# Probabilities transposed by 32x32 blocks on VectorE and by DMAs, with the attention stage in an order written out by hand

## The chip, the cores and the metric

The kernel runs on one NeuronCore of a Trainium2 chip, as one program. The metric is the device time of one execution in microseconds (us), shown as the median of several runs. Weights and activations come from the chip's main memory in 32-bit floats. The core's engines are PE (TensorE, matmuls and transposes), DVE (VectorE), ACT (ScalarE), POOL (GpSimd) and SP (SyncE, which here only issues DMAs). Each runs its own instruction list in order, and they wait for one another by semaphores.

## What is computed

Two encoder layers on `x` of shape (512, 1024). Three token mixers run side by side on one input projection, are scaled by gates and summed; an output projection, LayerNorm, a squared-ReLU MLP and a second LayerNorm follow.

```python
for layer in range(2):
    qa, ka, va, qb, kb, vb, qc, kc, vc, gate_logits = split(x @ w_in[layer])
    oa = dilated_attention(partial_rotary(qa) * scale, partial_rotary(ka), va)      # A: 4 heads of 64
    ob = axial_gqa(axial_rotary(rms_norm(qb)) * scale, axial_rotary(rms_norm(kb)), vb)   # B: 8 query heads, 2 k/v heads
    oc = neighbourhood_attention(qc * scale, kc, vc, rpb_c[layer])                  # C: 4 heads, 8 x 64 grid
    g = sigmoid(gate_logits + b_gate[layer])                                        # three gates of 1024
    mix = (g0 * (oa @ w_branch_a) + g1 * (ob @ w_branch_b) + g2 * (oc @ w_branch_c)) @ w_out
    x = layer_norm(ALPHA * x + mix)
    x = layer_norm(ALPHA * x + square(relu(x @ w_up)) @ w_down)
```

## The kernel before

**Matmuls.** Every operand is kept as a rounded part `hi` and a rest `lo` of 32-bit type fp32r, and `mm3` (lines 153 to 155) makes a product of three passes, hi*hi, hi*lo and lo*hi. Weights arrive in tiles of 128x1024 (`raw`, line 194). `Stream.split` makes `whi` on ACT (line 182) and `wlo = raw - whi` on DVE (line 183). Two `raw` tiles and up to five (in later stages eight) split tiles exist at a time, and `take` hands out the next one and advances the stream.

**The attention stage.** `attention` projects the queries and keys of mixer A, and then opens the stage that this case is about. Its outer loop runs over 64 *slots* a layer: 16 heads (four of A, four of C, eight of B) times four blocks `qb` of 128 queries. A slot has one block of scores, softmax, the transposition of its probabilities, and once a head the product with the values. Into each slot `work.pump(rate)` puts a share of matmuls that don't hang on it, twice: the projections of B and C, all gates of A and C, and the branch projections of A and C. So PE always has filler work. `rate` (2.1 for A, 2.85 for C, 1.6 for B) is the number of `mm3` of 512 columns that one call puts in. `chores` are pieces of head preparation (`prepare`, `norm_rotate`), of which `chores.pump` emits one or two at a time. Instructions of this stage are ordered by the framework's scheduler, from the order of the code.

**One slot.** `scores` (lines 513 and 514) multiplies q by the two parts of k into a bank `pss`. For A and C line 523 adds mask or bias and takes the maximum on DVE; for B line 519 does so by a reduction. Line 524 negates the maximum, line 525 is the exponential on ACT, line 528 the reciprocal of the sum on DVE, and line 529 scales the probabilities `p` by it, on POOL for A and B and on DVE for C. `turn` (line 544) transposes `p` in up to four 128x128 blocks on PE, by a product with `ident`, into a bank `psp`. `split_psum` (lines 228 and 229) writes `pth` on ACT and `ptl = psp - pth` on DVE. When the head's four slots are through, `values` (lines 558 and 559) multiplies the values by both parts. C's blocks see 256 or 384 keys, the others 512.

**Heads.** The matmul of the scores wants q split over both halves of the partitions (its `hi` in one, its `lo` in the other), and k whole in both halves. `head_k` (lines 446 and 447) writes both halves of `kh` on ACT and of `kl` on DVE, from the bank in which PE has transposed k.

**After the slots**, `tail` runs the gates and the projection of branch B, with the last head's `values` inside the first gate. Then come the output projection and the MLP, whose code the change leaves as it is but for the pool in which each weight tile is put.

PSUM has eight banks, dealt round by the pool: whatever bank is next is waited for, by `return psum.tile([P, 512], F32, tag="ps", name=name)`.

## Time and profile before

| | |
|---|---|
| median of 3 runs | 1547.56 us (1546.23 to 1547.92) |
| the profiled execution: its own time | 1549.4 us |
| its span, first to last instruction | 1547.6 us |
| busy: PE / DVE / ACT / POOL | 99% / 56% / 41% / 12% of the span |
| instructions | 19148 |
| DMA traffic | 150.61 MB, 97 GB/s over the span |

The span is what the rows below divide; 1.8 us of the execution lie outside it. An engine's idle time matters only where PE comes to wait for it. Matmuls overlap: one of 512 columns is shown with some 0.39 us, but the next starts 0.23 us later. The chain of waits counts each by what it adds.

### The profile page before, as it was taken

How to read it: one execution, taken by the hardware profiler on the slowest of the kernel's cores; microseconds unless marked ns; L12 is line 12 of the kernel's file. 1: busy time of each engine (PE TensorE's matmuls, PEld its weight loads, DVE VectorE, ACT ScalarE, POOL GpSimd, SP SyncE). 2: the span in 40 equal slices, each digit the busy share in tenths (PEclk: the TensorE clock that was granted, in tenths of full speed). 3: DMA queues.
4: the chain of work that ended last, by engine and by line, in shares of the span. 5: the costliest groups of instructions: out<-in, count | busy, mean ns of one | idle time of the engine just before them, and what ended most of it. 6: DMA issues, size and time to landing. Idle time of an engine off the chain costs nothing.

```text
span 1547.6 us, 19148 instructions
## 1 busy us (share of the span) xinstructions
PE 1527.6 (99%) x7400; PEld 1279.8 (83%) x7400; DVE 866.0 (56%) x1498; ACT 632.5 (41%) x1036; POOL 182.0 (12%) x190
## 2 busy tenths in 40 slices
PE   8999999999999999999999999999999999999997
PEld 6888888888898888888888888888888888888886
DVE  4678877644664314441566787776448542244315
ACT  4665666533144212431136556665332431134310
POOL 0113213211100000000102141233111000000001
PEclk9999999999999999999999999999999999999999
DMA  6222311153153323332331323112432432233311
GB/s 218 83 85 75 111 55 58 52 177 123 55 177 96 96 82 96 110 96 83 106 128 56 98 82 103 55 59 95 146 123 83 136 99 92 82 123 95 96 55 55
DMA packets 43434, 150.61 MB, mean 97 GB/s; under 512 B 5072, under 2 KB 5712, under 8 KB 43344
## 3 DMA queue, kind: packets, MB, share of 16 engines
q1 hardware_dynamic: 43344, 149.40, 30.5%
q8 instruction: 58, 0.95, 0.2%
q14 instruction: 32, 0.26, 0.1%
HBM read 145.19 MB, written 4.19 MB: 97 GB/s over the span
## 4 chain that ended last, share of the span: by engine, by line
PE 95%; DVE 2%; ACT 1%; DMA 1%; issue 0%; POOL 0%; SPq 0%; POOLq 0%; DVEq 0%; ACTq 0%
PE psd L155 9%; PE psd L154 9%; PE psd L153 9%; PE psu L154 8%; PE psu L155 8%; PE psu L153 8%; PE psg L155 6%; PE psg L154 6%; PE psg L153 6%; PE psp L544 3%; PE psq L155 2%; PE psq L153 2%; PE psq L154 2%; PE psb L155 2%; PE psb L153 2%; PE psb L154 2%
## 5 line engine op out<-in xcount | busy, mean ns | idle before, releaser
L183 DVE TENSOR_TENSOR wlo<-raw,whi 128x1024 fp32r<-128x1024 f32 (+1 forms) x246 | 306.9, 1248 | 421.5 <-ACT whi L182 420.5
L182 ACT ACTIVATE whi<-raw 128x1024 fp32r<-128x1024 f32 (+1 forms) x246 | 258.4, 1053 | 462.8 <-PE psd L155 143.1
L153 PE MATMUL psu<-xTh,whi 128*128 128x512 f32 (+1 forms) x576 | 210.8, 366 | 0.0
L154 PE MATMUL psu<-xTl,whi 128*128 128x512 f32 (+1 forms) x576 | 210.7, 366 | 0.0
L155 PE MATMUL psu<-xTh,wlo 128*128 128x512 f32 (+1 forms) x576 | 210.5, 365 | 0.0
L153 PE MATMUL psd<-whi,hh 128*128 128x512 f32 x512 | 199.3, 389 | 0.0
L155 PE MATMUL psd<-whi,hl 128*128 128x512 f32 x512 | 199.2, 389 | 0.0
L154 PE MATMUL psd<-wlo,hh 128*128 128x512 f32 x512 | 199.2, 389 | 0.0
L153 PE MATMUL psg<-xTh,whi 128*128 128x512 f32 x384 | 156.8, 408 | 0.0
L154 PE MATMUL psg<-xTl,whi 128*128 128x512 f32 x384 | 151.6, 395 | 0.0
L155 PE MATMUL psg<-xTh,wlo 128*128 128x512 f32 x384 | 151.6, 395 | 0.0
L154 PEld LDWEIGHTS psu<-xTl,whi 128*128 128x128 f32 x576 | 108.6, 189 | 17.7
L153 PEld LDWEIGHTS psu<-xTh,whi 128*128 128x128 f32 x576 | 108.6, 189 | 17.4
L155 PEld LDWEIGHTS psu<-xTh,wlo 128*128 128x128 f32 x576 | 108.6, 189 | 17.4
L266 POOL TENSOR_TENSOR ve<-ve,nhalf 128x1 f32<-128x1 f32 x16 | 24.2, 1513 | 775.0 <-DVE ve L265 775.0
L529 POOL TENSOR_SCALAR p<-p,stat 128x512 f32<-128x512 f32 x96 | 70.7, 737 | 360.2 <-DVE stat L528 242.9
L154 PEld LDWEIGHTS psd<-wlo,hh 128*128 128x128 f32 x512 | 96.1, 188 | 20.0
L153 PEld LDWEIGHTS psd<-whi,hh 128*128 128x128 f32 x512 | 96.1, 188 | 19.9
L155 PEld LDWEIGHTS psd<-whi,hl 128*128 128x128 f32 x512 | 96.1, 188 | 19.8
L153 PE MATMUL psq<-whi,xTh 128*128 128x512 f32 (+1 forms) x256 | 90.0, 351 | 7.2 <-ACT whi L182 6.7
L229 DVE TENSOR_TENSOR ptl<-psp,pth 128x512 fp32r<-128x512 f32 (+2 forms) x128 | 81.6, 637 | 21.2 <-ACT pth L228 19.8
L155 PE MATMUL psq<-whi,xTl 128*128 128x512 f32 (+1 forms) x256 | 87.9, 343 | 0.0
(116 smaller groups left out, 2572.7 us busy)
## 6 DMA issues: line engine op xcount, KB each, us to landing
raw<-in_w_up SPq DMA_DIRECT2D x64, 512.0 KB, 3.6
raw<-in_w_down SPq DMA_DIRECT2D x64, 512.0 KB, 3.5
raw<-in_w_gate SPq DMA_DIRECT2D x48, 512.0 KB, 3.5
raw<-in_w_qkv SPq DMA_DIRECT2D x22, 512.0 KB, 3.6
raw<-in_w_out SPq DMA_DIRECT2D x16, 512.0 KB, 3.6
raw<-in_w_c SPq DMA_DIRECT2D x12, 512.0 KB, 3.5
bias<-in_rpb SPq DMA_DIRECT2D x8, 640.0 KB, 3.9
raw<-in_w_bb SPq DMA_DIRECT2D x8, 512.0 KB, 3.6
```

The costliest lines, as they stand in the source:

```text
L153: nc.tensor.matmul(ps, lhs.hi, rhs.hi, start=start, stop=False)
L154: nc.tensor.matmul(ps, lhs.hi, rhs.lo, start=False, stop=False)
L155: nc.tensor.matmul(ps, lhs.lo, rhs.hi, start=False, stop=stop)
L182: nc.scalar.activation(hi[:, s], raw[:, s], AF.Copy)
L183: nc.vector.tensor_tensor(lo[:, s], raw[:, s], f32(hi[:, s]), op=ALU.subtract)
L229: nc.vector.tensor_tensor(dst.lo, ps, f32(dst.hi), op=ALU.subtract)
L266: nc.gpsimd.tensor_tensor(ve[:, 1:], ve[:, :1], nhalf[:, :1], op=ALU.pow)
L529: (nc.vector if name == "c" else nc.gpsimd).tensor_scalar(p, p, st[:, 3:4], 1.0, op0=ALU.mult, op1=ALU.mult)
L544: nc.tensor.transpose(ps[:, j * P:(j + 1) * P], p[:, j * P:(j + 1) * P], ident)
```

## The change

Probabilities are no longer transposed on PE. `turn` has DVE transpose each 32x32 block of `p` where it stands (one instruction a slot, into a tile `tx`), and `gather` moves the blocks to their partitions by 16 DMAs a head, each of 32 rows of 2 KB. The order of the 512 queries inside the result becomes (i, q, b), so `chosen`, `values` and `evict` use strided views. The tile that lands is the exact transposed matrix, so `settle` makes `hi` from it on ACT, in SBUF, and subtracts it in place on POOL (in the last head of a layer by turns on DVE). A head is settled two heads after it was scored, and its values are multiplied at the end of that time.

`head_k` writes one half only, and two DMAs copy it to the other. q and k are prepared head by head. The softmax takes the maximum negated, so line 524 goes; C's probabilities are scaled on POOL as the others. PSUM banks are dealt in groups by name: two for scores, three for `psk` and `psc`, three for the rest. The attention stage and the tail are emitted under `manual_schedule`, in the order of the code: `later`, `chain` and `catch_up` put PSUM evictions and the stream's splits at places in each slot. The rates become 2.2, 2.5 and 1.75. Split weight tiles are four (`AHEAD`) in each of two pools; the second pool is used in the first projection and by turns from the output projection on, so that the attention stage has four tiles instead of five. Of the plan of weights, the first tiles of C come ahead of B's k and v. The core of the diff:

```diff
-    psum = ctx.enter_context(tc.tile_pool(name="psum", bufs=8, space=bass.MemoryType.PSUM))
+    GROUPS = {"pss": (0, 2), "psk": (2, 5), "psc": (2, 5), None: (5, 8)}
...
+    def catch_up():
+        todo = soon[:]
+        soon.clear()
+        for f in todo:
+            f()
+        for c in chain[:]:
+            if next(c, None) is None:
+                chain.remove(c)
+        stream.advance()
...
-            for i in (h, 1 - h):
-                to = slice(i * HD, (i + 1) * HD)
-                nc.scalar.activation(dst(k.hi[to]), src(ps[own]), AF.Copy)
-                nc.vector.tensor_tensor(dst(k.lo[to]), src(ps[own]), dst(f32(k.hi[own])), op=ALU.subtract)
+            nc.scalar.activation(dst(k.hi[own]), src(ps[own]), AF.Copy)
+            yield 1
+            nc.vector.tensor_tensor(dst(k.lo[own]), src(ps[own]), dst(f32(k.hi[own])), op=ALU.subtract)
+            yield 1
+            for t in (k.hi, k.lo):
+                nc.sync.dma_start(f32(t)[other], f32(t)[own])
...
-            ps = bank("psp")[:, :n * P]
-            for j in range(n):
-                nc.tensor.transpose(ps[:, j * P:(j + 1) * P], p[:, j * P:(j + 1) * P], ident)
-            split_psum(pt[:, k0:k1, qb * P:(qb + 1) * P], ps.rearrange("p (k q) -> p k q", q=P))
+            nc.vector.transpose(squares[name, h][1][:, :, k0:k1, qb].rearrange("p j k b -> p k j b"),
+                                p.rearrange("p (k j a) -> p k j a", j=4, a=SQ))
+
+        def gather(name, h, ms, queues=(nc.sync,)):
...
+            for m in ms:
+                i, j = m % 4, m // 4
+                queues[m % len(queues)].dma_start(f32(lo)[j * SQ:(j + 1) * SQ, i],
+                                                  sq[i * SQ:(i + 1) * SQ, j].rearrange("a k q b -> a k (q b)"))
...
+        def settle(name, h, kbs, engines=(nc.gpsimd, nc.gpsimd)):
...
+            for kb in kbs:
+                q = keys_of(name, kb)
+                hi, lo = chosen(pt.hi[:, :, kb], *q), chosen(pt.lo[:, :, kb], *q)
+                nc.scalar.activation(hi, f32(lo), AF.Copy)
+                engines[kb % 2].tensor_tensor(lo, f32(lo), f32(hi), op=ALU.subtract)
...
-        rate = {"a": 2.1, "c": 2.85, "b": 1.6}
+        rate = {"a": 2.2, "c": 2.5, "b": 1.75}
...
+        with tc.manual_schedule():
...
+            for i, (name, h, qb) in enumerate(slots):
+                if i + 1 < len(slots):
+                    todo[i + 1].normalize()
+                score(i + 2)
+                turn(name, h, qb, todo[i].p)
+                if i >= 2 * TB and qb < 3:
+                    settle(*head_of(i - 2 * TB), ((0, 1), (2,), (3,))[qb])
+                catch_up()
+                soften(i + 2)
+                chores.pump()
+                work.pump(rate[name])
+                catch_up()
+                if i >= 2 * TB and qb == 3:
+                    values(*head_of(i - 2 * TB))
...
+                if i >= TB - 1:
+                    at = (i + 1) % TB
+                    gather(*head_of(i - at), range(4 * at, 4 * at + 4))
...
+            gather(*head_of(-1), range(4, 16), (nc.sync, nc.scalar))
+            settle(*head_of(-1 - TB), range(TB))
```

Over the two layers the program loses 464 transposes on PE, 128 subtractions `ptl`, 128 negations and 32 scalings of C on DVE, and 20 half copies of k each on ACT and DVE. It gains 128 block transposes on DVE, 124 subtractions, 32 scalings of C and 32 small fills of `tx` on POOL, 500 gathers and 40 copies of k among SP's DMAs, 12 gathers issued by ACT, and eight more evictions of C's outputs each on ACT and DVE.

How rows move, at three places of the B heads in the first layer. First PE, before, in one slot; `psb` is a branch projection, `psp` the transposition:

```order
L153 MATMUL psb_2665<-oh_1639,whi_2238 128x512 [waits PE_49]
L154 MATMUL psb_2665<-ol_1640,whi_2238 128x512
L155 MATMUL psb_2665<-oh_1639,wlo_2239 128x512
L544 MATMUL psp_2671<-ident_73,p_2587 128x128 [waits Pool_49]
L544 MATMUL psp_2671<-ident_73,p_2587 128x128 x3
L153 MATMUL psb_2665<-oh_2023,whi_2238 128x512
L154 MATMUL psb_2665<-ol_2024,whi_2238 128x512
L155 MATMUL psb_2665<-oh_2023,wlo_2239 128x512
```

And PE now, at the end of a head's last slot, `psg` being a gate's projection and `pso` the values of the head before the last:

```order
L184 MATMUL psg_2453<-xTh_80,whi_2268 128x512
L185 MATMUL psg_2453<-xTl_81,whi_2268 128x512
L186 MATMUL psg_2453<-xTh_80,wlo_2269 128x512
L646 MATMUL pso_2512<-pth_2402,v_808 128x512 [waits DVE_49,PE_49]
L646 MATMUL pso_2512<-ptl_2231,v_808 128x512 [waits DMAHW4_49,DMAHW3_49,DMAHW5_49,DMAHW2_49,DMAHW6_49,DMAHW1_49,DMAHW7_49,DMAHW0_49,Pool_49]
```

The transposes are gone and nothing stands in their place: PE's lists wait for POOL no longer in each slot, but once a head, at `values`. Second POOL, before (`p` is a scaling, `mg` the sum of the branches) and now:

```order
L617 TENSOR_TENSOR mg_1612<-mg_1612,t_2480 128x512 [waits DVE_49]
L529 TENSOR_SCALAR p_2549<-p_2549,stat_2550 128x512 [waits DVE_49,PE_49]
L529 TENSOR_SCALAR p_2587<-p_2587,stat_2588 128x512 [waits DVE_49,PE_49]
L529 TENSOR_SCALAR p_2630<-p_2630,stat_2631 128x512 [waits DVE_49,PE_49]
L617 TENSOR_TENSOR mg_1706<-mg_1706,t_2573 128x512 [waits DVE_49]
```

```order
L586 TENSOR_SCALAR p_2363<-p_2363,stat_2364 128x512 [waits DVE_49]
L632 TENSOR_TENSOR ptl_2231<-ptl_2231,pth_2402 128x4x128 [waits DMAHW3_49,DMAHW4_49,DMAHW2_49,DMAHW5_49,DMAHW1_49,DMAHW6_49,DMAHW0_49,DMAHW7_49,PE_49,Activation_49]
L632 TENSOR_TENSOR ptl_2231<-ptl_2231,pth_2402 128x4x128 [waits Activation_49]
L586 TENSOR_SCALAR p_2407<-p_2407,stat_2408 128x512 [waits DVE_49]
L632 TENSOR_TENSOR ptl_2231<-ptl_2231,pth_2402 128x4x128 [waits Activation_49]
L715 TENSOR_TENSOR mg_491<-mg_491,t_2260 128x512 [waits DVE_49]
```

Between the scalings of one head stand four subtractions of 128x512 that were DVE's. Third SP now, where a weight tile (`raw`) stood alone with the next one before:

```order
L226 DMA raw_2374<-in_w_gate 128x1024 [waits DMAHW7_49,DVE_49]
L616 DMA ptl_2385<-tx_2245 32x512 [waits DMAHW0_49,PE_49]
L616 DMA ptl_2385<-tx_2245 32x512 [waits DMAHW1_49]
L616 DMA ptl_2385<-tx_2245 32x512 [waits DMAHW2_49]
L616 DMA ptl_2385<-tx_2245 32x512 [waits DMAHW3_49]
```

The first gather of a head waits for the values of the head whose `ptl` it overwrites, and each DMA for the one eight issues earlier (`DMAHW0` to `DMAHW7`); the weight tiles queue with them.

## Rows read from the trace of the kernel before

**Rows 1.** The page's first part: busy time of each engine.

```profile
PE 1527.6 (99%) x7400; PEld 1279.8 (83%) x7400; DVE 866.0 (56%) x1498; ACT 632.5 (41%) x1036; POOL 182.0 (12%) x190
```

**Rows 2.** Whom PE waited for: us in total, times, longest.

```profile
PE psq L153 <- ACT whi L182: 6.7, 1, 6.7
PE psp L544 <- POOL p L529: 4.6, 2, 2.3
```

**Rows 3.** Stages of A, C, B slots: us of PE, PEld, DVE, ACT, POOL.

```profile
53.10:122.80 69.70, 69.70 (x382) 59.85 (x383) 49.44 (x121) 41.86 (x84) 10.34 (x15) 0.98 0.25 78
122.80:199.90 77.10, 77.10 (x387) 64.80 (x386) 62.94 (x150) 46.40 (x92) 23.23 (x23) 1.00 0.30 93
199.90:301.25 101.35, 101.35 (x505) 83.49 (x504) 76.59 (x153) 60.98 (x118) 29.32 (x35) 1.00 0.17 53
```

**Rows 4.** Chain that ended last: start, us added, what.

```profile
199.90 0.44 PE psp L544 x4
200.33 0.23 PE psg L153
...
301.25 0.44 PE psp L544 x4
```

**Rows 5.** As rows 3, around both layers' first transposition; the granted clock follows POOL.

```profile
51.00:52.00 1.00, 0.00 (x0) 0.00 (x0) 1.00 (x6) 0.70 (x2) 0.68 (x1) 1.00 0.69 274
54.00:55.00 1.00, 1.00 (x4) 0.81 (x3) 0.59 (x1) 0.37 (x1) 0.36 (x1) 0.50 0.91 348
800.00:825.00 25.00, 22.67 (x145) 20.52 (x145) 16.30 (x40) 14.66 (x31) 3.67 (x4) 0.93 0.37 114
```

**Rows 6.** Groups by line: count | busy us, mean ns | idle before.

```profile
L183 DVE TENSOR_TENSOR wlo<-raw,whi 128x1024 fp32r<-128x1024 f32 (+1 forms) x246 | 306.9, 1248 | 421.5 <-ACT whi L182 420.5
L229 DVE TENSOR_TENSOR ptl<-psp,pth 128x512 fp32r<-128x512 f32 (+2 forms) x128 | 81.6, 637 | 21.2 <-ACT pth L228 19.8
L519 DVE TENSOR_REDUCE stat<-pss 128x1 f32<-128x512 f32 x64 | 43.8, 685 | 3.7 <-PE pss L514 3.3
L524 DVE TENSOR_SCALAR stat<-stat 128x1 f32<-128x1 f32 x128 | 19.1, 151 | 2.5
L382 DVE TENSOR_TENSOR rw<-rw,ss 128x640 f32<-128x640 f32 x8 | 6.6, 823 | 6.7 <-POOL ss L380 6.7
```

**Rows 7.** POOL's lines: duration ns min/median/max, first and last start.

```profile
L617 POOL TENSOR_TENSOR mg<-mg,t x32: 1270/1290/2204, 234.7 to 1143.8; 128x512 f32<-128x512 f32 x32
L529 POOL TENSOR_SCALAR p<-p,stat x96: 687/696/1711, 51.3 to 1071.3; 128x512 f32<-128x512 f32 x96
L389 POOL TENSOR_TENSOR t<-rw,cs x32: 315/740/1590, 138.9 to 932.2; 128x256 f32<-128x256 f32 x16, 128x64 f32<-128x64 f32 x16
```

**Rows 8.** Timeline: start us, duration, instruction, at two places.

```profile
266.58 1.29 POOL L617 TENSOR_TENSOR mg<-mg,t 128x512 f32<-128x512 f32 x1 [3.27 <-DVE t L607]
267.08 1.86 DVE L183 TENSOR_TENSOR wlo<-raw,whi 128x1024 fp32r<-128x1024 f32 x1
...
310.68 1.22 DVE L183 TENSOR_TENSOR wlo<-raw,whi 128x1024 fp32r<-128x1024 f32 x1
310.85 2.20 POOL L617 TENSOR_TENSOR mg<-mg,t 128x512 f32<-128x512 f32 x1 [4.23 <-DVE t L607]
```

**Rows 9.** Line 183 alone in the stages of rows 3: DVE us, count.

```profile
122.80:199.90 77.10, 13.41 (x11) 1.00 0.30 93
199.90:301.25 101.35, 14.26 (x11) 1.00 0.17 53
```

**Rows 10.** SP's queue in time, then DMAs by size and us to landing.

```profile
9.70 0.43 SPq L651 DMA_DIRECT2D hb<-in_b_gate  x1
21.86 0.33 SPq L194 DMA_DIRECT2D raw<-in_w_gate  x1
...
x_dram<-x SPq DMA_DIRECT2D x8, 256.0 KB, 2.0
ropea<-in_rope_a SPq DMA_DIRECT2D x1, 64.0 KB, 7.1
```

More of the change, by code (lines that the diff above doesn't have):

```diff
@@ L720, in attention @@
-        work.flush()
-        stream.plan([a for m in range(KB) for a in g(1, [m]) + ([w_bb[l, m // 2]] if m % 2 == 0 else [])])
-        def tail():
-            steps = 0
-            for m in range(KB):
-                for _ in gated("b", m):
-                    steps += 1
-                    if steps == 4:
-                        values(*slots[-1][:2])
+            while key == ("b", 0) and "b" not in flags:
+                chores.step(False)
+            if key == ("b", 0) and "b0" not in flags:
+                chores.add(make_pair("b", 0))
```

365 lines of the change are left out of this document (238 added, 127 removed).

## Prediction

> **What bounds the kernel now.** First the busy times: PE is busy for 1527.6 of 1547.6 us, the next engine, DVE, for 866.0, and POOL for 182.0 [rows 1]. Then whom PE waited for. The list has two entries of weight: 6.7 us for the first weight tile of the program, which the change leaves as it is (SP issues the same first DMAs in the same order), and 4.6 us in two waits for POOL's scaled probabilities, one per layer, before its first transposition [rows 2]. By stage PE is busy all through the slots of A, C and B (69.70 of 69.70, 77.10 of 77.10, 101.35 of 101.35 us) [rows 3]. So time can come out only where PE's own list gets shorter or its few waits go, and it is lost wherever another engine becomes late enough for PE to feel it.
>
> **PE's part.** The chain gives four transpositions 0.44 us, the slower start of the matmul behind them included, where a matmul of 512 columns adds 0.23 us [rows 4]. That is 0.11 us for one. 464 of them go: 464 x 0.11 = 51.1 us. Nothing replaces them on PE; the values' matmuls keep their number and columns.
>
> With them goes the wait for POOL, since PE now meets the probabilities two heads later. It was 2.3 us in each layer [rows 2], and it cost more than itself: the granted clock was still 1.00 in the idle stretch and 0.50 in the stretch behind it, so 1.2 instead of 2.4 GHz [rows 5]. In the second layer's 25 us around the same place the clock averages 0.93, which is 0.07 x 25 = 1.7 us lost [rows 5]. I take 4.6 + 2 x 1.7 = 8.0 us for both layers.
>
> **The slot as it becomes.** Slots were 69.70/16 = 4.36 us (A), 77.10/16 = 4.82 (C) and 101.35/28 = 3.62 (B; seven of eight heads lie in the stage) [rows 3]. Without transpositions, and with two calls of the new rates at 3 x 0.23 = 0.69 us per `mm3`, they are 4.36 - 0.44 + 0.14 = 4.06 (A), 4.82 - 0.28 - 0.48 = 4.06 (C, 2.5 transpositions on average), and 3.62 - 0.44 + 0.21 = 3.39 (B). The rates only move filler between stages. The other engines have to fit into these.
>
> **DVE.** It spends 76.59/28 = 2.74 us in a slot of B [rows 3]. It loses `ptl`, 0.64, and the negation, 0.15 [rows 6], and gains a block transposition of 128x512, which no row shows. Lower bound: the copy-like `ptl`, 0.64; upper bound: two passes of the reduction over the same columns, 2 x 0.685 = 1.37 [rows 6]. One pass from SBUF is nearest to the reduction, so I take 0.685: 2.64 of 3.39 us, hidden. In a slot of C it had 62.94/16 = 3.93 us of 4.82, 82%, without a wait of PE [rows 2, 3], and loses about as much as it gains. The halves of k that go and the extra evictions of C are a few passes a head and stay under that cover. If the cover goes, each microsecond per slot costs 64 us in B alone.
>
> **ACT.** 60.98/28 = 2.18 us per slot of B [rows 3]; the copy that makes `hi` now reads SBUF, but stays one pass. Hidden by 1.2 us.
>
> **POOL** takes the subtraction. It had 29.32/28 = 1.05 us per slot of B [rows 3]; a subtraction of two SBUF operands of this size is line 617's, 1.29 at the median [rows 7]. So 2.34 of 3.39 us. The values need it one slot after the last piece is emitted, so a late piece costs nothing at first.
>
> **POOL and DVE together.** The timeline shows that they hold each other up. POOL's sum beginning at 266.58 takes 1.29 us, and the `wlo` that starts at 267.08, inside it, takes 1.86; at 310.68 `wlo` came first with 1.22, and the sum that starts at 310.85 takes 2.20 [rows 8]. In both, the one that came second ran as long as if it had waited for the first to end. The Trainium skill, SBUF — State Buffer, section "SBUF: two separate sides", says that a VectorE instruction with two SBUF inputs and a GpSimd instruction that reads SBUF take a shared pair of ports by an exclusive lock for the whole instruction; the trace agrees with it here, and by the rule as by the rows the sum below holds; if the two engines ran freely, its 4 us would go and I would expect 1492. So their times are to be added. In B: 2.34 + 14.26/28 for `wlo` [rows 9] = 2.85 of 3.39 us, which fits. In C: POOL's 23.23/16 = 1.45 [rows 3], the scaling of C at 320 of 512 columns 0.44, eight subtractions of A and eight of C 16.8/16 = 1.05 [rows 7], `wlo` 13.41/16 x 5.0/5.7 = 0.74 [rows 9], and three passes over 640 columns for each of four blocks of B's queries, 3 x 4 x 0.82/16 = 0.62 [rows 6]. That is 4.30 of 4.06 us; with a fill a slot, which has no row and is at most half a scaling (0.35), 4.65. C's stage is overbooked by 0.24 to 0.59 us a slot, 3.8 to 9.4 us a layer. Two heads of lag take up some of it. From 0 to 9.4, I take 2 us a layer, 4 in all, nearer the lower end since the lag is longer than that backlog.
>
> **SP.** A head of B lasts 4 x 3.39 = 13.6 us and brings 16 gathers at 0.43 us of issue and about two weight tiles at 0.33: 7.5 us [rows 10]. Landing is bounded by 2.0 us (256 KB between memories) and 7.1 us [rows 10]; the last gather is emitted two slots, 6.8 us, before it is used. Hidden at either end. A gather in front of a weight tile holds it while it waits for its head's transposition or its lane, a slot at most, and a tile is split three half slots after its issue at the earliest. I cost it at nothing, with that cover. The same holds for k's other half, except in the first head of a layer.
>
> **Two new waits of PE.** Scores have two banks, so the third block at the start of each layer's slots waits for DVE's first maximum: at most one pass, 0.69; I take 0.5, so 1.0 us. And B's query projection holds four weight tiles, now all there are: the tile behind it can be split only when the first is given back. At worst PE waits for two passes like `wlo`'s 1.25 us [rows 6], 2.5 us; at best not at all, as three more tiles' matmuls stand in between. I take about the middle, 1.2 a layer, 2.4 us.
>
> **Sum**, against the profiled execution's own 1549.4 us: 1549.4 - 51.1 - 8.0 + 4.0 + 1.0 + 2.4 = 1497.7. The median of the runs, 1547.56, lies 1.8 us under that execution, so I expect **1496 us**.
>
> **Rivals.**
> *POOL and DVE in turns fill C's stage* and PE feels all of it: 2 x 9.4 = 18.8 in place of 4, so 1511 us. For it: 4.65 us of work in 4.06 us slots, and that a wait of over 2 us halves the clock for a while [rows 5]. Against: the fill reads nothing, and B's slots leave room to catch up. This is the exclusive lock of the Trainium skill's page SBUF — State Buffer, section "SBUF: two separate sides", at its full price; the timeline agrees as far as it shows two such meetings.
> *The block transposition takes two passes*, 1.37 us. DVE then has 3.32 of 3.39 us in B, and with some 0.4 `wlo` a slot held up by 0.63 us each, as in the timeline [rows 8], 3.57: 64 x 0.18 = 12 us, so 1508. For it: output in pieces of 32 columns; against: reductions and copies in any view here are one pass.
> *POOL becomes the bound, slower than before.* The subtraction works in place on a strided view of four pieces, which no row shows. Line 389 works in strided views; its longest, 1.59 for at most 256 columns, would be 3.18 for 512 [rows 7]. A slot of B then has 1.05 + 3.18 + 0.51 = 4.74 us of POOL's and DVE's work in turn; 64 x 1.35 = 86 us over, so 1582. It decides from 2.64 us for one subtraction, where 64 x 0.81 us eat up the 52 gained. Against: its median of 0.74 makes it 1.48, and line 617's 1.29 is the nearest.
> That the change doesn't do what it says is excluded: PE's list has no transposition of probabilities left.
>
> **How the numbers follow.** My forecast has 0.56: the terms that carry it have rows. The filled stage of C has 0.18, two passes 0.10, POOL 0.16. What a measurement here can tell from no change is about 0.2%, 3 us. The first three are all faster, 0.84; of POOL's 0.16, 0.03 falls within 0.2% and 0.13 is slower. The range leaves out POOL's case alone: its lower end is the sum without any new wait, 1549.4 - 59.1 - 1.8 = 1488.5, less those 3 us, 1485; its upper end has the filled stage and two passes at once, 1496 + 14.8 + 12 = 1523.
>
> **What would show it.** Right: PE's list of waits still has nothing of weight but the first tile, POOL is busy for some 2.3 us a slot of B, DVE's block transposition takes about 0.7 us, and the clock stays at 1.00 at both layers' first slots. The filled stage: PE idle in C's slots, behind `wlo` or scaled probabilities, with POOL's subtractions well above 1.3 us. POOL: PE waiting at `values` for line 632, POOL at over 90% in B. Wrong altogether: PE waiting for gathers or for weight tiles that land late.

## The result, and the profile after

The changed kernel takes **1597.97 us** (median of 4 runs, 1594.96 to 1599.44), the kernel before beside it 1547.74 (1546.23 to 1550.53): a ratio of 1.032, 95% interval 1.030 to 1.034. That is 50 us slower where some 51 us faster was predicted, and far above the predicted range (1485 to 1523). Ahead of the detail: PE's own work came out near its forecast, and what was forecast to be hidden was not.

PE's busy time in the profiled execution (span 1597.6), to be read beside [rows 1]:

```profile
PE 1516.1 (95%) x6936; PEld 1251.1 (78%) x6936; DVE 837.5 (52%) x1330; ACT 619.2 (39%) x1024; POOL 352.3 (22%) x378
```

The 464 transposes are gone, but PE is now idle for 1597.6 - 1516.1 = 81.5 us (20.0 before), and no other engine is over 52%. So over the whole span no engine has become the bound by its load. Whom PE waited for, where [rows 2] had two entries of weight:

```profile
PE psc L184 <- DVE qs L502: 11.9, 2, 7.0
PE psg L184 <- ACT t L688: 10.5, 6, 2.5
PE psb L184 <- DVE of L668: 7.0, 2, 3.6
PE psq L184 <- ACT whi L214: 6.4, 1, 6.4
PE psb L184 <- ACT mg L688: 5.9, 2, 3.0
...
PE psg L184 <- DVE of L668: 3.7, 2, 1.9
PE pso L646 <- POOL ptl L632: 3.6, 7, 0.5
```

Most of these are a new kind of wait. PE wants to begin a product (`psc`, `psg`, `psb`: a projection of C, a gate, a branch) and its PSUM bank is not yet free: DVE or ACT has still to evict an earlier one. The five rows whose releaser is `qs`, `t`, `of` or `mg` make 39.0 us. The values' wait for POOL's subtraction, the rival that I had feared, is 3.6.

The stages of the first layer's slots, A, C and B as in [rows 3] and with its columns (us, then PE, PEld, DVE, ACT, POOL busy, granted clock, DMA share, GB/s), and two short stretches out of B's:

```profile
48.40:108.00 59.60, 52.62 (x269) 44.93 (x270) 36.55 (x82) 30.81 (x63) 15.93 (x19) 0.94 0.55 131
108.00:188.00 80.00, 72.27 (x311) 58.59 (x311) 57.97 (x126) 42.57 (x88) 55.06 (x72) 0.94 0.56 153
188.00:301.00 113.00, 99.77 (x421) 79.14 (x419) 73.45 (x130) 61.58 (x126) 54.62 (x59) 0.95 0.48 119
...
254.70:257.20 2.50, 0.00 (x0) 0.00 (x0) 2.09 (x5) 2.35 (x6) 2.50 (x4) 1.00 0.80 142
258.50:261.00 2.50, 2.50 (x7) 1.94 (x7) 2.33 (x3) 0.63 (x2) 0.06 (x1) 0.50 0.24 36
```

PE is busy for 88 to 90% of every stage, at a granted clock of 0.94 or 0.95 where it had been 0.98 to 1.00. From the start of a layer's first score to that of its last, which is called the slots from here on, the first layer takes 271.0 us (256.8 before); from there to the first product of the output projection, the tail, 85.3 us (74.3 before). Over both layers that is 26.3 us more in the slots and 21.8 in the tails, 48.1 of the 50.0 us by which the two profiled spans differ. The last two lines are one of the waits: while PE stands still (0.00 of 2.50 us), the clock is still 1.00 and DVE, ACT and POOL are nearly full; in the stretch behind it PE runs at 0.50, so at 1.2 GHz.

How one wait comes about, in the timeline (start, duration), and below it how the slots end:

```profile
252.44 0.39 PE L186 MATMUL psg<-xTh,wlo 128*128 128x512 f32 x1
...
252.69 0.60 ACT L498 ACTIVATE qs<-psk 64x512 fp32r<-64x512 f32 x1
...
253.32 1.15 ACT L631 ACTIVATE pth<-ptl 128x512 fp32r<-128x512 f32 x2
...
253.46 0.71 DVE L604 STREAM_TRANSPOSE tx<-p 128x512 f32<-128x512 f32 x1 [0.60 <-PE psg L186]
...
254.10 0.65 DVE L574 TENSOR_REDUCE stat<-pss 128x1 f32<-128x512 f32 x1
...
254.85 0.69 ACT L582 ACTIVATE p<-pss,stat 128x512 f32<-128x512 f32 x1 [0.38 <-DVE stat L574]
...
255.53 0.58 ACT L665 ACTIVATE of<-pso 64x512 f32<-64x512 f32 x1
...
256.00 0.62 ACT L631 ACTIVATE pth<-ptl 128x512 fp32r<-128x512 f32 x1
...
256.52 0.67 ACT L688 ACTIVATE t<-psg,hb 128x512 f32<-128x512 f32 x1
...
257.25 0.50 PE L184 MATMUL psg<-xTh,whi 128*128 128x512 f32 x1 [2.55 <-ACT t L688]
...
313.67 18.50 SPq L616 DMA_DIRECT2D ptl<-tx  x26
...
328.89 2.19 ACT L631 ACTIVATE pth<-ptl 128x512 fp32r<-128x512 f32 x4 [7.95 <-DMA ptl<-tx]
...
332.27 1.03 SPq L226 DMA_DIRECT2D raw<-in_w_gate  x2
...
336.19 1.06 ACT L214 ACTIVATE whi<-raw 128x1024 fp32r<-128x1024 f32 x1 [4.48 <-DMA raw<-in_w_gate]
...
337.29 0.80 PE L184 MATMUL psg<-xTh,whi 128*128 128x512 f32 x1 [1.85 <-ACT whi L214]
```

A gate's last matmul starts at 252.44. Its eviction `t` starts only at 256.52, since ACT's list puts in front of it a part of q, three copies `pth`, an eviction `of`, and an exponential; and that exponential waits for DVE's maximum, which stands behind the block transposition on DVE. This wait of ACT is only 0.38 us: here it is mostly the work put ahead of `t` that makes it late, on an engine that is busy for 39% of the span. PE has three banks for such products, runs out of them, and waits 2.55 us. At the end of the slots it is SP's turn: 26 gathers in a row take 18.50 us, the first two tiles of the tail stand behind them, and ACT waits 7.95 us for a gather and 4.48 for the first tile.

The new operations by line (count | busy us, mean ns):

```profile
L632 POOL TENSOR_TENSOR ptl<-ptl,pth 128x512 fp32r<-128x512 f32 (+2 forms) x124 | 155.3, 1264 | 25.4 <-ACT pth L631 23.5 <-PE pso L646 0.4 <-PE pss L567 0.4
...
L604 DVE STREAM_TRANSPOSE tx<-p 128x512 f32<-128x512 f32 (+2 forms) x128 | 82.7, 646 | 9.3 <-PE pso L646 4.8 <-DMA ptl<-tx 1.5 <-POOL p L586 0.9
```

Both cost what was taken for them (1.29 us from [rows 7] and 0.685 from [rows 6]). The prediction didn't fail on the price of an instruction of DVE or POOL.

### The profile page after: what moved, and what is told of

Read it like the earlier page. It is cut to its first block, busy times and chain, and to the rows that moved or that the text cites. A ratio compares the mean times of both kernels' runs of the same rounds, so it can differ in the third digit from the quotient of the medians.

```text
span 1597.6 us, 19273 instructions
## 1 busy us (share of the span) xinstructions
PE 1516.1 (95%) x6936; PEld 1251.1 (78%) x6936; DVE 837.5 (52%) x1330; ACT 619.2 (39%) x1024; POOL 352.3 (22%) x378
## 4 chain that ended last, share of the span: by engine, by line
PE 67%; DVE 11%; ACT 8%; DMA 5%; issue 5%; SPq 2%; POOL 1%; ACTq 0%; POOLq 0%; DVEq 0%
PE psd L184 9%; PE psd L186 9%; PE psd L185 9%; PE psu L185 7%; PE psu L184 7%; PE psu L186 7%; PE psg L184 3%; PE psg L186 3%; ACT whi L214 3%; ACT p L582 3%; PE psg L185 3%; DVE wlo L215 3%; DMA ptl<-tx 2%; SPq L616 2%; PE pso L646 2%
## 5 line engine op out<-in xcount | busy, mean ns | idle before, releaser
L632 POOL TENSOR_TENSOR ptl<-ptl,pth 128x512 fp32r<-128x512 f32 (+2 forms) x124 | 155.3, 1264 | 25.4 <-ACT pth L631 23.5
L186 PE MATMUL psg<-xTh,wlo 128*128 128x512 f32 x384 | 156.5, 407 | 0.1
L185 PE MATMUL psg<-xTl,whi 128*128 128x512 f32 x384 | 155.7, 405 | 0.0
L586 POOL TENSOR_SCALAR p<-p,stat 128x512 f32<-128x512 f32 (+2 forms) x128 | 87.8, 686 | 302.2 <-DVE stat L585 273.5
L184 PEld LDWEIGHTS psg<-xTh,whi 128*128 128x128 f32 x384 | 75.9, 198 | 38.0 <-ACT t L688 13.2
```

The costliest lines, as they stand in the source:

```text
L184: nc.tensor.matmul(ps, lhs.hi, rhs.hi, start=start, stop=False)
L185: nc.tensor.matmul(ps, lhs.hi, rhs.lo, start=False, stop=False)
L186: nc.tensor.matmul(ps, lhs.lo, rhs.hi, start=False, stop=stop)
L586: nc.gpsimd.tensor_scalar(self.p, self.p, self.st[:, 3:4], 1.0, op0=ALU.mult, op1=ALU.mult)
L632: engines[kb % 2].tensor_tensor(lo, f32(lo), f32(hi), op=ALU.subtract)
```

## The experiments

Three theories were set up from this profile. **1**: the banks are dealt in groups that are too small. **2**: in the written order DVE and ACT serve softmax, transposition and evictions in one serial loop. **3**: the 512 gathers, 500 of them issued by SP, delay probabilities and weights. Later come **5**, the written order as a whole, and **6**, four weight tiles for five. Each time is a median of 4 runs (6 in the last), each ratio to runs of the kernel before on the same chip; waits, slots and tails are those of one profiled execution.

### One part of the order, the banks or the gathers at a time

**Banks.** From B's heads on:

```diff
+    LATE = {"pss": (0, 2), "psk": (2, 4), "psc": (2, 4), None: (4, 8)}
```

> From the place where the first pair of B's heads is prepared to the end of a layer's slots, the group of PSUM banks for transposed k and q shrinks from three to two and the group 'rest' (gates, branches, values) grows from three to four; all else is as in the changed kernel. Theory 1 (the banks were dealt too small: PE waits for an eviction of the bank it wants next): the waits of psg and psb for lines 688 and 668, 11.9 us in the B slots of the first layer and some 12 in the second, go or fall under 6 in all, and with them a part of the half-clock stretches behind them; 1565 to 1580 us, while the 7 and 5 us of psc in A's slots stay. Theory 2 (ACT and DVE run a serial loop through the softmax, and every eviction comes out late by as much as the engines are behind): one bank more only puts the wait off, 1588 to 1600. Theory 3 (SP's gathers are the limit): no change, 1595 to 1602.

Measured: 1602.71 us, ratio 1.035 (1.034 to 1.037), above all three ranges. The first layer's last score is multiplied at 310.3 us in place of 317.6, so the slots did get shorter. But its output projection begins at 403.3 (402.9 in the changed kernel): PE now waits in the tail.

```profile
PE psg L186 <- DVE of L670: 22.0, 3, 15.2
PE psg L186 <- ACT whi L216: 13.0, 1, 13.0
```

So the second run kept the groups through the tail, and planned its tiles ahead:

```diff
+        for m in range(KB):
+            stream.plan(g(1, [m]) + [w_bb[l, i] for i, at in enumerate((2, 3, 5, 7)) if at == m])
         cp = [c_pair(0), c_pair(1)]
```

> As in the run with four banks for the rest from B's heads on, but the four stay to the end of the layer's branch B, and the weights of branch B's tail are planned ahead of the slots, so that their DMAs stand before the last head's gathers. In the first such run PE reached the end of its work in the slots 13 us earlier in the first layer, and then waited 13.0 and 15.2 us for the tail's first tile. Theory 1 (small groups of banks cost what PE waits for in B's slots): these waits go, 26 to 30 us and a part of the half-clock stretches behind them, so 1565 to 1578. If the slots' own end is set by the chain of softmax, gathers and copies of the last heads (theories 2 and 3), PE waits there for something else instead: 1588 to 1603.

Measured: 1603.85 us, 1.037 (1.035 to 1.038). The two long waits in the tail (13.0 and 15.2 us) are gone, and another has come:

```profile
PE pss L568 <- ACT p L584: 14.1, 6, 3.6
```

A score's matmul now waits for the exponential that holds one of its two banks: PE has caught up with the softmax itself. `psc`, `psg` and `psb` still wait 31.1 us for evictions (39.0 in the changed kernel). Theory 1 falls as the cause: in these two runs a bank more only changes what PE waits for.

**The place of the reciprocal.**

```diff
-                if i + 1 < len(slots):
-                    todo[i + 1].normalize()
                 score(i + 2)
                 turn(name, h, qb, todo[i].p)
+                if i + 1 < len(slots):
+                    todo[i + 1].normalize()
```

> The only edit: in each slot the transposition of block i on DVE, the settling and the first round of evictions come ahead of the reciprocal and the scaling of block i+1, which waits for ACT's exponential. Theory 2 (in-order DVE stands before that reciprocal while evictions and the transposition, which are ready, are queued behind it): waits of PE for evictions fall by half or more, from 43 us to under 20, and the time to 1560 to 1580. Theory 1 (only the number of banks counts): the waits stay, 1590 to 1602. A loss is possible too: POOL gets its scaling later, and the transposition of the next slot waits for that; then DVE waits for POOL in the next slot and the time is 1600 to 1625.

Measured: 1590.95 us, 1.028 (1.026 to 1.029): 7 us less, where theory 2 hoped for 18 to 38. `psc` still waits 10.7 us, `psg` 10.1 for `t`. The text above says more than the edit does: only the transposition went ahead of the reciprocal, while settling and evictions still stand behind it. So it is the weaker test of theory 2.

**The place of the weight split.**

```diff
-                catch_up()
+                catch_up(False)
                 soften(i + 2)
+                stream.advance()
```

> In the first half of each slot the split of the next weight tile (whi on ACT, wlo on DVE, 1.05 and 1.23 us) comes behind the softmax's maximum and exponential instead of ahead of them. Theory 2 (a serial loop: the maximum stands behind wlo, wlo waits for whi, whi stands behind the copies of the settling, and the exponential waits for the maximum; ACT waits 224 us in 107 waits for a maximum): ACT's waits for maxima fall by a third or more and the time to 1570 to 1588. Theory 1 or 3: no change, 1592 to 1602; a weight tile split later could also make PE wait for whi, up to 1610.

Measured: 1618.04 us, 1.046 (1.044 to 1.047), the wrong way by 20 us and outside every range. My reading of which instruction holds up which was wrong here; moving a split by one place in the lists cost 20 us. These two runs show that the time hangs on the order, not that I knew the better one.

**The scheduler's order** for the slots (`nullcontext()` in place of `tc.manual_schedule()`):

> The slot loop is ordered by the framework's scheduler as in the kernel before, not in the order of the code; the tail keeps the written order, the groups of banks, the four weight tiles and the gathers stay. Theory 5 (the written order is what costs): the waits of PE fall to a few us and the time to 1500 to 1540. Theory 1 (banks): the order in which banks are dealt is fixed by the code either way, so the waits stay within a third of 43 us, 1580 to 1610. Theory 3 (SP): the same, 1585 to 1610.

Measured: 1644.33 us, 1.062 (1.061 to 1.064), above every range given. In A's slots PE was busy for 72.00 of 72.00 us at clock 1.00, as predicted for the change; but the tail waited 15.7 and 15.9 us for its first tile, and the values 28.4 us for POOL. Three more runs followed: the tail's tiles planned early, then also one ring of eight banks, then also the tail scheduled.

> The slots ordered by the scheduler, as in the earlier run of that kind (1644.33 us), and the weight tiles of branch B's tail planned ahead of the slots. In that run PE had no idle time in A's slots (72.00 of 72.00 us, clock 1.00), and lost 15.7 us in the first layer's tail and 15.9 in the second's on the first tile of the tail, then ran the stretch at a mean clock of 0.84. If the late plan is the cause: both waits go and part of the clock's loss, 32 to 50 us, so 1594 to 1612. If the tile is late because SP is full of gathers there, the wait stays or moves to another tile: 1625 to 1645.

> As the run beside it with the early plan, and the eight PSUM banks in one ring as in the kernel before, in place of groups of 2, 3 and 3. Theory 1 (small groups cost, and the scheduler could only not help that): PE's waits in C's and B's slots for DVE, ACT and POOL fall by more than half, the time to 1540 to 1575. If the groups don't matter: within 10 us of the run beside it. Theory 3 (SP): the same as that.

> As the one with the ring of eight banks, and the tail too is ordered by the scheduler, so that of the change stay the transposition on DVE and by DMAs, POOL's subtraction, half of k by DMA, four tiles and the rates. My prediction of 1496 had summed just these. If the written order and the groups were what it lacked: 1500 to 1540. If the transposition's own chain (DVE, 16 gathers on SP, copy on ACT, subtraction on POOL, then the values) holds PE up in any order: 1560 to 1620, and PE's list of waits is led by the values' matmuls waiting for POOL, ACT or a gather.

Measured: 1624.00, 1623.67 and 1620.90 us (1.049, 1.048, 1.046, each within 0.002). The early plan gave 20 us, less than the 32 to 50 it was said to give; the ring, which by theory 1 should have given most, nothing. The last run comes out as its second case says (1560 to 1620, 0.9 us over): the chain holds PE up in this order too. In the last of them the list of waits and a piece of the timeline read:

```profile
PE pso L643 <- POOL ptl L629: 36.6, 47, 3.4
PE pso L643 <- ACT pth L628: 16.8, 8, 4.0
```

```profile
309.28 2.18 ACT L628 ACTIVATE pth<-ptl 128x512 fp32r<-128x512 f32 x4
...
309.95 0.65 PE L643 MATMUL pso<-pth,v 128*128 128x512 f32 x1 [2.00 <-ACT pth L628]
...
311.64 3.46 POOL L629 TENSOR_TENSOR ptl<-ptl,pth 128x512 fp32r<-128x512 f32 x2
...
312.96 0.79 PE L643 MATMUL pso<-ptl,v 128*128 128x512 f32 x1 [2.35 <-POOL ptl L629]
```

The scheduler puts a head's four settlings directly ahead of its values, and PE, in order, stands before them. Here the wait at the values that my third rival spoke of does come, though POOL's subtraction, 1.73 us each in these two, takes 1.251 in the mean of the run, no longer than forecast. In this run scores also wait 7.3 us for the copied half of k, which the prediction had called hidden, and gates 12.9 us for a weight tile; without the chain, below, PE's list has neither.

**The gathers**, doubled and reduced:

```diff
+                for _ in range(2):
+                    queues[m % len(queues)].dma_start(f32(lo)[j * SQ:(j + 1) * SQ, i],
```

> Every gather is issued twice (500 more DMAs of 64 KB on SP, 0.6 us of issue each, and 32 MB more moved). Theory 3 (SP's queue and the DMAs it delays are what costs): the queue gets 150 us more of issue in each layer's 280 us of slots, so weight tiles and probabilities land later and PE waits for whi of late tiles and for ptl: 1640 to 1720 us. Theories 1 and 2 (banks, loop of ACT and DVE; SP has slack): at most a few more us, 1595 to 1612, and the list of PE's waits names the same evictions.

Measured: 2524.41 us, 1.632 (1.629 to 1.635). As a price it says little: the second copy of a pair writes where the first does, and SP waits for the first to land each time, which no theory had priced:

```profile
SPq L617 <- DMA ptl<-tx: 783.0, 495, 5.1
```

It does agree with the way from a late gather to PE: ACT's `pth` waits 878.2 us for gathers, and the gates 206.6 us for the eviction `t`, which is ACT's too.

```diff
-                queues[m % len(queues)].dma_start(f32(lo)[j * SQ:(j + 1) * SQ, i],
-                                                  sq[i * SQ:(i + 1) * SQ, j].rearrange("a k q b -> a k (q b)"))
+                queues[j % len(queues)].dma_start(f32(lo)[:, j], sq[:, j].rearrange("a k q b -> a k (q b)"))
```

> The 16 gathers a head (64 KB each, 32 rows) become four copies of 128 rows and 256 KB, issued at the places where four gathers stood. The bytes, the places and the waits stay; the blocks are not moved to their partitions, so this leaves out the exchange of partitions between blocks (the values are formed from probabilities in the wrong rows). It takes 12 of 16 issues from SP: at 0.6 us some 7 us of each head's 17.6. Theory 3 (SP's issues are the limit, since SP is busy for 85% of the B slots, and late probabilities and weights hold ACT, whose evictions are then late): PE's waits for evictions fall by more than half, and the time to 1530 to 1565. Theories 1 and 2 (banks, order of ACT and DVE): not over 10 us gained, 1588 to 1600, with the same evictions in PE's list of waits.

Measured: 1578.30 us, 1.020 (1.018 to 1.022): 20 us less with the same bytes in a quarter of the issues, in neither of the two ranges. The waits for evictions stay (`psc` 11.8 us, `psg` 10.6). The slots of the first layer are only 3 us shorter; 7 more come out of the tail (78.1 us), whose first tiles no longer stand behind 18.50 us of gathers; in the second layer it is 2.4 and 6.8. So theory 3 is right for the slots' end, and not for their middle.

**Four weight tiles** in the kernel before:

```diff
-                if self.used[more] == (5, 3)[more]:
+                if self.used[more] == (4, 3)[more]:
```

> The kernel before with four split weight tiles at a time in place of five, as the changed kernel has them in the attention stage, all else as before (so four also in its first projection and in its MLP's first pool). If the fifth tile is worth much to the attention stage (theory 6), 1560 to 1580 and PE waits for whi in the slots; if not, as predicted (1.2 us a layer), 1547 to 1553. Theories 1 to 3 need this to be small.

Measured: 1554.94 us, 1.0052 (1.0034 to 1.0071). From the first score to the first product of the output projection it takes 332.5 and 332.1 us in the two layers (331.1 and 331.0 before), so the stage in question loses 2.5 of the 7.7 us, near the 2.4 predicted. These are single executions, and that of this run is 4.3 us above its median, so 2.5 is a rough size. It is far from the 12 us or more of theory 6, and PE has no wait for `whi` in the slots: theory 6 falls.

**PE's transposes in the written order**, with the banks and the plan of the second bank run. The transposed blocks take turns with the scores in the two banks `pss`, and the values come one head later:

```diff
+            ps = bank("psp")[:, :n * P]
+            for j in range(n):
+                nc.tensor.transpose(ps[:, j * P:(j + 1) * P], p[:, j * P:(j + 1) * P], ident)
+            later(lambda: split_psum(dst, ps.rearrange("p (k i b) -> p k i b", i=4, b=SQ)))
```

> The written order, with four banks for the rest from B's heads on and the early plan, but the probabilities transposed on PE again (into a bank of the scores' group) and split from there by ACT and DVE; values one head later in place of two, no gathers, no subtraction of probabilities on POOL. Beside 1603.85 us with the block transposition in the same order. By PE's own list this adds 51 us, 1655, if PE is the bound; if the transposition's chain is what makes the waits (theory 3 and POOL), the waits go and it is 1575 to 1615; if the written order and the banks make them (theories 1, 2, 5), waits for evictions stay above 30 us and it is 1635 to 1670.

Measured: 1665.14 us, 1.075 (1.074 to 1.077), in the range for order and banks. It decides less than it was meant to, since the shared banks make a wait of their own (a score waiting for an exponential, 52.7 us in 39 waits; 14.1 in the run beside it).

### Taking the chain away, link by link

By now one part after another had been tried, and none gave the loss back. So the transposition's chain (`turn`, `gather` and `settle`: all that stands between the scaled probabilities and the values) was left out piece by piece, with PE's matmuls unchanged throughout.

```diff
+        def turn(*_):
+            if not parts:
+                parts["all"] = Split(*(pool.tile([P, 4, TB, P], F32R, tag=f"tx{n}", name="still", bufs=1) for n in range(2)))
+                for t in (parts["all"].hi, parts["all"].lo):
+                    nc.gpsimd.memset(f32(t), 0.0)
+
+        def gather(*_):
+            pass
...
+        def settle(*_):
+            pass
...
-            pt = parts.pop((name, h))
+            pt = parts['all']
```

> The same left out of the kernel whose slots and tail the scheduler orders, with one ring of eight banks and the early plan of the tail's tiles (1620.9 us with the chain). Its list of PE's waits was led by the values' matmuls, waiting 36.6 us for POOL's subtraction and 16.8 for ACT's pth. If that is all that the chain costs there: 1500 to 1515 (my 1496, and the some 7 us that the kernel before lost with four weight tiles). If above 1530, something else in the changed code than order and chain costs, k's half by DMA, the rates or the way of the evictions.

> The changed kernel without its transposition: no block transposition on DVE, no gathers, no copy to pth on ACT, no subtraction on POOL; the values multiply one tile of zeros. PE's list, the written order, the groups of banks, the softmax and the four weight tiles stay. It leaves out everything between scaled probabilities and the values. If the transposition's chain makes PE's waits: 1496 to 1510, with the evictions gone from PE's list of waits. If the written order of the softmax and the evictions with its small groups of banks makes them whatever the chain does (theories 1, 2, 5): 1550 to 1585, with psc, psg and psb still waiting for evictions for over 25 us.

With the scheduler's order **1495.18 us**, 0.966 (0.964 to 0.968), just under its lowest range; with the written order 1534.04, 0.991 (0.990 to 0.992), between its two ranges, so that the chain and the order each make a part. The waits of PE, scheduler's order first:

```profile
PE psq L181 <- ACT whi L211: 6.6, 1, 6.6
PE psr L183 <- DVE wlo L212: 4.4, 2, 2.2
```

```profile
PE psb L184 <- DVE of L644: 7.9, 2, 4.0
PE psq L184 <- ACT whi L214: 6.7, 1, 6.7
PE psc L184 <- DVE qs L502: 6.3, 2, 4.3
...
PE psg L184 <- ACT t L664: 1.5, 2, 0.8
```

Then the chain was put back in the written order: the block transposition alone (`turn` kept, `gather` and `settle` empty), transposition and gathers (`settle` empty, the values multiplying `ptl` twice).

> The changed kernel with its block transpositions on DVE (128 of 0.65 us, 83 us of DVE's time) and the fills of tx, but without gathers and settling; the values multiply a tile of zeros. So it leaves out what brings the transposed blocks to the values. It stands between 1534.04 us (no chain at all) and 1595.26 (transposition and gathers, no settling). If the transposition itself, in order on DVE behind POOL's scaling and ahead of the evictions, is the link that costs: 1570 to 1595, with PE's waits for evictions as in the changed kernel. If the gathers are (500 issues on SP in front of the weight tiles, 32 MB more to move): 1534 to 1550, and the waits as without the chain.

> The changed kernel without the settling: the 128 copies to pth on ACT (0.62 us) and the 128 subtractions (1.26 us on POOL) are left out, and the values multiply the landed tile twice. So neither ACT nor POOL waits for a gather any more, PE alone does. If it is the settling, with its waits for gathers (22.1 us on ACT) and POOL's load, that makes evictions late: 1540 to 1570. If theory 2 holds (maximum, exponential, reciprocal and splits in turn on DVE and ACT): ACT's part of the loop gets 0.62 us a slot shorter, 10 to 25 us in all, 1572 to 1588. If neither: 1590 to 1600.

The first of the two measured 1560.18 us, between its two ranges, and the second 1595.26, in the range for neither settling nor theory 2.

| written order, but for the first | us | PE busy | PE idle | clock | slots | tails |
|---|---|---|---|---|---|---|
| no chain, scheduler's order, ring of banks, early plan | 1495.18 | 1473.4 | 20.4 | 0.997 | 453.8 | 153.2 |
| no chain | 1534.04 | 1485.8 | 46.8 | 0.991 | 490.1 | 153.0 |
| and block transposition on DVE | 1560.18 | 1492.8 | 69.1 | 0.986 | 518.1 | 153.2 |
| and gathers | 1595.26 | 1497.6 | 95.7 | 0.978 | 518.8 | 186.7 |
| and settling: the change | 1597.97 | 1516.1 | 81.5 | 0.974 | 539.9 | 170.3 |

(Idle is the span less the busy time of the profiled execution; slots and tails are of both layers together.) So the written order with its groups and late plan costs 38.9 us, the transposition 26.1, the gathers 35.1, the settling 2.7. The last two columns say where: order and transposition lengthen the slots and not the tails, the gathers the tails and hardly the slots. The late plan by itself costs nothing, since without gathers the tails are equal with it and without it. The settling's 2.7 hides 21.1 us more in the slots and 16.4 less in the tails. These are steps in this sequence, not prices that hold in another one: under the scheduler the whole chain costs 1620.90 - 1495.18 = 125.7 us, in the written order 63.9.

What DVE's transposition does to PE:

```profile
PE psc L184 <- DVE qs L502: 12.3, 2, 7.0
PE psb L184 <- DVE of L654: 9.4, 2, 4.7
...
PE psg L184 <- ACT t L674: 6.4, 6, 1.6
PE pss L566 <- DVE qs L502: 5.2, 2, 2.7
```

These are the waits that are there without it, longer: `psc` 12.3 for 6.3, `psg` 6.4 for 1.5. ACT's waits for DVE's maxima, too, grow, from 247.4 to 275.1 us, while the block transposition itself waits only 0.9 us for POOL's scaling. With the gathers one is added, in the tail, 14 us a layer:

```profile
PE psg L184 <- ACT whi L214: 28.6, 2, 14.5
```

```profile
304.11 20.08 SPq L616 DMA_DIRECT2D ptl<-tx  x26
324.29 6.44 SPq L226 DMA_DIRECT2D raw<-in_w_gate  x3
...
328.07 1.06 ACT L214 ACTIVATE whi<-raw 128x1024 fp32r<-128x1024 f32 x1 [16.81 <-DMA raw<-in_w_gate]
...
329.18 0.80 PE L184 MATMUL psg<-xTh,whi 128*128 128x512 f32 x1 [14.06 <-ACT whi L214]
```

SP issues the tail's first tile only when 26 gathers have kept it for 20.08 us. This wait is 28.6 us, beside 35.1 between the medians. Settling adds only 2.7, because it fills just this stretch: with it PE reaches the end of the slots 10 us later (last score 317.6 against 308.0) and no longer waits there. The output projection begins at nearly the same time (402.9 and 401.5). So the 2.7 doesn't say that settling is cheap: its 21.1 us in the slots are in the 10 to 25 that theory 2 gave for it, and the tail hides most of them. This is the tail's tile behind the gathers, as the run with fewer issues had shown from the other side.

**No scaling.**

```diff
-                nc.vector.reciprocal(self.st[:, 3:4], self.st[:, 2:3])
-                nc.gpsimd.tensor_scalar(self.p, self.p, self.st[:, 3:4], 1.0, op0=ALU.mult, op1=ALU.mult)
+                pass
```

> The changed kernel without reciprocal and scaling: the probabilities are transposed as the exponential leaves them (128 scalings on POOL of 0.69 us and 128 reciprocals on DVE of 0.16 us are left out). DVE's first instruction in each slot, which waits for ACT's exponential (42.1 us in 61 waits), is gone, and the transposition no longer waits for POOL. Theory 2: ACT and DVE run further apart, PE's waits for evictions halve, 1560 to 1580. Theory 1 (banks) or 3 (gathers): at most 8 us, 1589 to 1600.

Measured: 1579.46 us, 1.021 (1.019 to 1.022). 18.5 us go with two short instructions a slot, so the time is just inside theory 2's range. But the waits did not halve: `psc` (7.1 us), `psb` (13.2) and `psg` (11.9) still wait 32.2 us for evictions, where it had been 39.0. PE's idle time fell by only 3.5 us and its busy time by 15.9, at a clock of 0.983 for 0.974. Theory 2's size is borne out here, its mechanism only in part.

**A faster kernel**, with what stood firm: the wait at the first slots, ended in the kernel before.

```diff
         ahead(1)()
+        work.pump(4)
...
-            work.pump(rate[name])
+            work.pump(rate[name] - 0.5 * (i < TB))
```

> The kernel before with PE's transpositions, and four of the filler's matmul triples moved from the first head's slots to the place ahead of the first slot, so that PE has work while the first probabilities are scaled. My prediction gave 8.0 us to the end of that wait (4.6 us of PE's waiting for POOL in two places, and 3.4 of clock behind it). If that term was right: 1538 to 1542. If the wait only moves (to a score's matmul or a weight tile): 1545 to 1549.

Measured: **1542.62 us**, ratio 0.9966 (0.9954 to 0.9978): 0.3% less than the kernel before, clear of the noise, and 0.6 us above the range given.

```profile
PE psp L544 <- POOL p L529: 1.7, 2, 1.0
```

```profile
800.00:825.00 25.00, 23.97 (x147) 20.90 (x146) 18.07 (x45) 15.77 (x32) 3.48 (x5) 1.00 0.34 106
```

The wait fell from 4.6 to 1.7 us and the clock there from a dip of 0.93 [rows 5] to 1.00: 5.2 us for 2.9 us of waiting.

## Why the prediction was wrong, point by point

- **PE's part was right.** Without the 4.0 us for POOL and DVE in turn the sum was 1496 - 4 = 1492; the kernel without the chain, in the scheduler's order, measures 1495.18. The parts agree too, and not only the sum: its PE is busy for 54.2 us less than before (51.1 for the transposes and 3.4 of clock were taken, 54.5), and idle for 20.4 us (20.0 - 4.6 + 1.0 + 2.4 = 18.8 by the terms). It is not the changed kernel, though, but PE's list of it. Of the small terms, the third score block's wait for its bank (1.0 taken) has 0.4 in the changed kernel's list of waits, and four weight tiles (2.4 taken) show 2.5 in the kernel before and, in the kernel without the chain, a wait of 4.4 (`psr`) right behind B's query projection. The term for the first slots, 8.0 us, is borne out in its mechanism: 5.2 for 2.9 of 4.6 us of wait.
- **The step that failed** is the one that fitted the other engines' busy times into the new slot lengths: "2.64 of 3.39 us, hidden" for DVE, and "I cost it at nothing, with that cover" for SP. A busy time under the slot's length shows that an engine can keep up on average. It doesn't show that the one instruction PE waits for comes out in time, when it stands in order behind others that wait in their turn for ACT, DVE or a DMA. The block transposition, of the size taken (0.646 for 0.685 us), cost 26.1 us there. For C's slots the cover was not even there on paper: DVE's 3.93 us were set against the old slot of 4.82, and are 97% of the prediction's own new slot of 4.06. ACT's copies were called hidden by 1.2 us a slot in the same way; settling, of which they are a part, lengthened the slots by 21.1 us.
- **The gathers** were priced at 0.43 us from a small load of the first instructions [rows 10]. SP took 0.588 at the median and 18.50 us for 26 at the end of the slots, 0.71 each. The cover was counted in slots before the data are used; what else stands behind them on SP, the first tiles of the tail, which are planned only after the slots, I had named for the middle of the stage and not for its end. They cost 35.1 us, and the tails are 33.5 us longer with them, the slots 0.7.
- **The written order and the groups of banks had no term**, but for the two banks of the scores. They cost 38.9 us without any chain, nearly all in the slots (36.3). How much of that is order and how much the groups isn't shown, since the written order wasn't run with one ring of banks; under the scheduler the ring changed nothing. That the scheduler puts PE's other products in front where the written list stops is a likely reason, and not shown either.
- **Each wait cost more than itself.** From the kernel without the chain in the scheduler's order to the change PE's idle time grows by 81.5 - 20.4 = 61.1 us and the busy time for the same 6936 matmuls by 42.7. The fall of the mean clock from 0.997 to 0.974 makes some 35 of these, by an estimate from the two clocks (1473.4 x 0.997 / 0.974). The prediction had seen this at one place (4.6 us of waits, 3.4 of clock) and put it on the side of the gain.
- **The rivals.** POOL as the bound, the only slower one, was wrong in its mechanism: its subtraction took 1.264 us, not 2.64, PE waited 3.6 us for it, and POOL was busy for 48% of the first layer's B stage, where over 90% had been its sign. How the settling's 21.1 us in the slots divide between ACT's copies and POOL's subtractions isn't shown. The filled stage of C came only in small part: of PE's 7.73 us of waiting in the first layer's C slots 1.8 stand behind `wlo` and none behind scaled probabilities. The two-pass transposition is excluded by its 0.646. The range (1485 to 1523) had no case in which evictions come late, though the prediction's last line named weight tiles that land late as what would make it wrong altogether, and gave it no chance.

What stays open: which order would hide the chain, and why it costs twice as much under the scheduler (125.7 us) as in the written order (63.9). Two edits of the written order moved the time by -7 and +20 us, so the 38.9 and 26.1 are prices of this order. Wider groups from A's slots on, and the early plan with the changed kernel's own banks, weren't tried. That PE would wait for nothing with the chain in some order is not shown.

## What to carry to other kernels

Before work is called hidden, list for each eviction that frees a bank, and each tile that PE takes next, what stands in front of it in order on its engine, and what those wait for; slack in busy time says nothing about that. The test that separates the two is cheap: leave the new chain out, keep PE's matmuls, and time it in both orders. Here that gave 1495 for PE's part and 39 + 64 us for order and chain, where the edits of single parts had given no answer. Read each step by stage too: the settling looked like 2.7 us, and was 21 in one stage less 16 in the next. And a queue that many small DMAs go through needs its own row, at its end above all: what is planned behind the last of them starts late by their sum.

## What the hardware showed that was not expected

A copy of 32 rows of 2 KB inside SBUF took SP 0.588 us to issue (median of 500), the straight copies of 128 rows and four times the bytes 0.591 (median of 124), a weight tile of 512 KB from main memory 0.33. The Trainium skill, DMA: Bandwidth & Descriptors, section "Issuing engines are not separate DMA queues", calls the time to initiate a DMA usually small beside the transfer. For one copy the trace agrees, 0.588 us against 2.8 from issue to landing (median). But issues add up on one queue: 26 of them in a row kept SP for 18.50 us, and what was planned behind them came late by that.

```profile
L616 SPq DMA_DIRECT2D ptl<-tx x500: 507/588/1576, 67.0 to 1121.0; - x167
```

```profile
ptl<-tx SPq DMA_DIRECT2D x500, 64.0 KB, 2.8
```
